# Reordering the steps of the delta-rule inverses and of attention among the matrix products of a two-layer hybrid mixer

## The chip, the cores and the metric

The kernel runs on one core of one Trainium2 chip. The metric is device time in microseconds (us) for one execution of the whole program, which is two layers and the final norm. The kernel before takes 1586.25 us, the median of three runs (1586.24 to 1587.02).

The engines are named as in the profile: PE multiplies matrices, PEld loads its weights, DVE is the vector engine, ACT the scalar engine, POOL the general one, SP issues DMAs. Each engine works through its own list of instructions in the order in which the built program holds them, and waits on semaphores for the others.

## The reference, cut to what matters

Two layers of a backbone over 256 latent tokens and 256 context tokens of width 1024. Each layer projects the normalised tokens once into column groups that feed three mixers: a Fourier branch, a bidirectional gated delta rule, and differential attention. The mixers are projected, merged by gates, and followed by a squared-ReLU MLP. The change touches the order of the work of two mixers.

```python
# delta rule, per chunk of 64 tokens, head and direction
gcum = jnp.cumsum(g, axis=-1)
decay = jnp.exp(jnp.where(lower, gcum[..., :, None] - gcum[..., None, :], -jnp.inf))
lmat = jnp.where(strict, jnp.einsum('nbhid,nbhjd->nbhij', kb, kc) * decay, 0.0)
tmat = lax.linalg.triangular_solve(eye + lmat, eye, left_side=True, lower=True, unit_diagonal=True)
u = tmat @ (vc * bc)
w = tmat @ (kb * jnp.exp(gcum)[..., None])
qk = jnp.einsum('nbhid,nbhjd->nbhij', qc, kc) * decay
def step(s, xs):
    v_new = u_i - w_i @ s
    out = qd_i @ s + qk_i @ v_new
    s = s * jnp.exp(gl_i)[..., None, None] + jnp.einsum('bhcd,bhce->bhde', ke_i, v_new)
# differential attention
s = jnp.einsum('bqhmd,bkhmd->bhmqk', q, k) * (DA_QK_DIM ** -0.5)
p = jax.nn.softmax(s, axis=-1)
a = p[:, :, 0] - lam * p[:, :, 1]
o = jnp.einsum('bhqk,bkhe->bqhe', a, v)
```

## The kernel before

**Dense products.** Nearly all of PE's time goes to weight products in float32 that are split into a high and a low half (`whi`, `wlo`, cast by ACT at L254 and subtracted by DVE at L255; the tokens are `hh`, `hl`), three products for each tile (`mm3`). They need no result of the chains below, and so can stand between the steps of a chain while ACT and DVE prepare the next step.

**Weave and chains.** `Weave` counts the time of these products as they are emitted (`weave.time`, columns divided by 2400 a microsecond, four passes for float32) and remembers, for each, its place in the scheduler's priorities. A chain of dependent small steps is emitted later inside `weave.chain()`: `at(t)` gives all that follows the priority of the product that stood at product time `t`. A step at `t0 + lat` thus goes `lat` microseconds of products behind the step at `t0`, and past the last product it simply follows. The scheduler then settles each engine's order, by these priorities and by what is ready in its own model.

**The delta-rule chain.** Four heads are taken as two pairs, in two layers: four chains, `dn_chain`, each with a step distance `lat` from `LAT` (1.2 and 1.0 us in layer 0, 0.6 and 0.6 in layer 1). A chain calls `prepare` twice, for two of its four chunk steps each, and then `step` four times. `prepare` has three parts. `products` multiplies k by k and k by q and copies the result to `gq` (DVE L663, ACT L666). Then, for each of its two steps `i`, come the decay: eight ACTIVATEs write the log rows `rh` and `rl` (L713, one buffer each), five products turn them into differences in a bank `pd` (`negr`, `rh`, `rl`), ACT takes the exponential `dec` (L721), DVE makes `C32` with four instructions (L723), ACT casts it to `C16` (L725, both are shown as `C` in the trace), POOL adds the identity, and DVE multiplies `dec` by `gq`. Last, at `2 * lat`, seven levels of a recursive inverse: the products of `C16` with `Tm`, DVE's mask `X` (L745), the products of `X` with `Um`, DVE's sum into `Tm` (L754), a transposition on PE and ACT's copy `Um` (L758); after the levels `T32`, `E16` and `U32` refine the result (L763 to L776). `step` forms `R`, multiplies it by `U32`, and makes `vs`, `vn`, the output and the new `state`.

**Attention.** `attention` handles a head in three groups of queries (two in layer 1). For each it places the scores (`km`, `q`), `CORE[0]` = 2.4 us later four transposes of `pe` and ACT's copy `aT` (L1045), `CORE[1]` = 0.8 us later the products of `aT` with the values `vt` and ACT's copy `od` (L1051), and after `CORE[2]` = 0.6 us the next group; at the end the norm of `od` (DVE L1061), its transposes and `yh`, `yl`.

**Beside them** in layer 0, pair 0 and in layer 1, pair 0 the Fourier branch `fnet` runs: its result banks are split into `u` (ACT and DVE L275, L276) and multiplied with the cosine table `ct`.

Of the kernel before, what the change touches and what calls it, by code (L numbers as in the profile page):

```python
# [11 lines left out]
F32 = mybir.dt.float32  # L12
F32R = mybir.dt.float32r
F16 = mybir.dt.float16
I32 = mybir.dt.int32
AF = mybir.ActivationFunctionType
# [18 lines left out]
LAT = ((1.2, 1.0), (0.6, 0.6))  # L35
POST = (5.0, 4.0)
GATE = (1.0, 9.0)
CORE = (2.4, 0.8, 0.6, 5.0)
NRM = (1.4, 3.0)

EARLY = 3
# [140 lines left out]
def body(tc, A, dbg=None):  # L182
    nc = tc.nc
    weave = Weave(tc)
    V, S, G, PE = nc.vector, nc.scalar, nc.gpsimd, weave
# [177 lines left out]
    tri = [kc[:, K_TRI + d * P:K_TRI + (d + 1) * P] for d in range(2)]  # L363
# [102 lines left out]
    def mixer(l, last, front):  # L466
# [11 lines left out]
        gates = {}  # L478
# [170 lines left out]
        def dn_chain(p, q2, k2, ktm, vtm, since, lat):  # L649
# [4 lines left out]
            def products(t):  # L654
                ps = dbank()
                withq = t < 2 or not last
                for h in range(2):
                    kt_ = k2[:, h, t * P:(t + 1) * P]
                    PE.matmul(ps[:, h * P:(h + 1) * P], kt_, kt_, start=True, stop=True)
                    if withq:  # L660
                        PE.matmul(ps[:, (2 + h) * P:(3 + h) * P], kt_, q2[:, h, t * P:(t + 1) * P], start=True, stop=True)
                o = dp.tile([P, 4, P], F32, tag="gq", name="gq", bufs=2)
                V.tensor_tensor(out=o[:, 0:2], in0=ps[:, 0:256].rearrange("p (a b) -> p a b", b=P),  # L663
                                in1=kc[:, K_NOT:K_NOT + P].unsqueeze(1).broadcast_to([P, 2, P]), op=ALU.mult)
                if withq:
                    S.copy(o[:, 2:4], ps[:, 256:512].rearrange("p (a b) -> p a b", b=P))  # L666
                return o

            def quad(nm, dt=F32, bufs=1, w=P):
                return dp.tile([P, 4, w], dt, tag=nm, name=nm, bufs=bufs)  # L670
# [17 lines left out]
            units = [(d, h) for d in range(2) for h in range(2)]  # L688

            def prepare(steps, t0):  # L690

                def at_(t):
                    nonlocal t0
                    t0 += t
                    at(t0)

                def part(t, i):

                    return t.rearrange("p (d s h) b -> p d s h b", d=2, s=2)[:, :, i]

                want = FWD[steps[0]] < 2 or not last
                at_(0)
                gq = {t: products(t) for t in sorted(FWD[s] for s in steps)}
                at_(lat)
                C32, C16 = (dp.tile([P, 8, P], t_, tag=nm, name=nm) for t_, nm in ((F32, "C32"), (F16, "C16")))
                decs = []
                for i, s in enumerate(steps):
                    tiles = (FWD[s], BWD[s])
                    rh, rl = quad("rh", F32R), quad("rl", F32R)
                    for u, (d, h) in enumerate(units):  # L710
                        for r_, g_ in ((rh, gates["ghi"].bitcast(F32)), (rl, gates["glo"])):
                            g_ = g_[:, d, s, 2 * p + h:2 * p + h + 1]
                            S.activation(r_[:, u], tri[d], AF.Copy, scale=g_)  # L713
                    pD = dbank()
                    PE.matmul(pD.rearrange("p (d h b) -> p d h b", d=2, b=P), idr, negr.unsqueeze(2).broadcast_to([P, 2, 2, P]), start=True, stop=False)
                    for d in range(2):
                        for j, r_ in enumerate((rh, rl)):
                            PE.matmul(pD[:, d * 256:(d + 1) * 256], strir[:, d], flat(r_)[:, d * 256:(d + 1) * 256],
                                      start=False, stop=d == 1 and j == 1)
                    dec = quad("dec", F32, 3)  # L720
                    S.activation(flat(dec), pD, AF.Exp)  # L721
                    for u, (d, h) in enumerate(units):
                        V.scalar_tensor_tensor(out=C32[:, 4 * d + 2 * i + h], in0=gq[tiles[d]][:, h],  # L723
                                               scalar=beta[:, d, s, 2 * p + h:2 * p + h + 1], in1=dec[:, u], op0=ALU.mult, op1=ALU.mult)
                    S.copy(part(C16, i), part(C32, i))  # L725
                    G.tensor_tensor(out=part(C32, i), in0=part(C32, i),
                                    in1=ident.unsqueeze(1).unsqueeze(1).broadcast_to([P, 2, 2, P]), op=ALU.add)
                    if want:
                        for d in range(2):
                            V.tensor_tensor(out=dec[:, 2 * d:2 * d + 2], in0=dec[:, 2 * d:2 * d + 2], in1=gq[tiles[d]][:, 2:4], op=ALU.mult)  # L730
                    decs.append(dec)


                at_(2 * lat)
                Tm, Um = (dp.tile([P, 8, P], F16, tag=nm, name=nm) for nm in ("Tm", "Um"))
                G.tensor_copy(Tm, id8)
                G.tensor_copy(Um, id8)
                for lv_ in range(NLVL):
                    w_ = 1 << lv_
                    tc_, uc_ = every_second(Tm, w_, 0), every_second(Um, w_, 1)  # L740
                    pX = dbank()
                    for u in range(8):
                        PE.matmul(pX[:, u * 64:(u + 1) * 64], C16[:, u], every_second(Tm, w_, u // 4, u), start=True, stop=True)
                    X = dp.tile([P, 8, 64], F16, tag="X", name="X")
                    V.tensor_tensor(out=X.rearrange("p (d h) b -> p d h b", d=2), in0=pX.rearrange("p (d h b) -> p d h b", d=2, b=64),  # L745
                                    in1=lvl[:, lv_].unsqueeze(2).broadcast_to([P, 2, 4, 64]), op=ALU.mult)
                    new = flat(X)
                    at_(lat)
                    if lv_:
                        new = dbank()  # L750
                        for u in range(8):
                            PE.matmul(new[:, u * 64:(u + 1) * 64], Um[:, u], X[:, u], start=True, stop=True)
                        at_(lat)
                    V.tensor_tensor(out=tc_, in0=new.rearrange("p (d b c) -> p d b c", d=2, c=w_), in1=tc_, op=ALU.add)  # L754
                    pU = dbank()
                    for u in range(8):
                        PE.matmul(pU[:, u * 64:(u + 1) * 64], Tm[:, u], every_second(id16, w_, 1 - u // 4, 0), start=True, stop=True)
                    S.copy(uc_, pU.rearrange("p (d b c) -> p d b c", d=2, c=w_))  # L758
                index = [[4 * d + 2 * i + h for d, h in units] for i in range(2)]
                pRs, U32s = [], []  # L760
                for i in range(2):
                    T32 = quad("T32", F32)
                    S.copy(T32.rearrange("p (d h) b -> p d h b", d=2), part(Tm, i))  # L763
                    pR = dbank()
                    for u, v in enumerate(index[i]):
                        PE.matmul(pR[:, u * P:(u + 1) * P], C32[:, v], T32[:, u], start=True, stop=True)
                    pRs.append(pR)
                for i in range(2):
                    at_(lat)
                    E16 = quad("E16", F16)  # L770
                    V.tensor_tensor(out=E16, in0=ident.unsqueeze(1).broadcast_to([P, 4, P]), in1=b4(pRs[i]), op=ALU.subtract)
                    pR = dbank()
                    for u, v in enumerate(index[i]):
                        PE.matmul(pR[:, u * P:(u + 1) * P], E16[:, u], Um[:, v], start=True, stop=True)
                    U32 = quad("U32", F32, 3)
                    V.tensor_tensor(out=U32.rearrange("p (d h) b -> p d h b", d=2), in0=pR.rearrange("p (d h b) -> p d h b", d=2, b=P),  # L776
                                    in1=part(Um, i), op=ALU.add)
                    U32s.append(U32)
                at_(lat)
                return t0, [(U32s[i], decs[i], want) for i in range(2)]  # L780
# [222 lines left out]
        def attention(h, qk, ap_, gain, cos, sin):  # L1003

            q, km, t0 = qk
            vt = vals[h]
            t0 = max(t0 + CORE[3], core_end[0])
            weaving = weave.chain()
# [4 lines left out]
            for ts in ((0,), (1,), (2, 3))[:2 if last else 3]:  # L1013
# [22 lines left out]
                for i in range(ng):  # L1036
                    sl = slice(i * wt, (i + 1) * wt)
                    V.scalar_tensor_tensor(out=pe[:, 0, sl], in0=pe[:, 1, sl], scalar=z[:, i:i + 1], in1=pe[:, 0, sl], op0=ALU.mult, op1=ALU.add)
                t0 += CORE[0]
                at(t0)  # L1040
# [61 lines left out]
        at_ = attention_pool()  # L1102
# [410 lines left out]
```

## Time and profile before

| what | value |
|---|---|
| median of the three runs | 1586.25 us |
| the profiled execution | 1584.71 us, of which its span is 1582.6 us |
| PE busy | 1517.0 us, 96% of the span |
| PEld, DVE, ACT, POOL busy | 82%, 74%, 46%, 9% |
| granted TensorE clock, mean | 0.99 of full speed |

The profiled execution lies 1.54 us below the median. PE is busy in nearly every slice of the span, but the ends of matmuls are modelled, so that short waits can hide in its busy time; what PE waited for is read from the list of waits and, place by place, from the timeline, where the bracket behind an instruction gives the idle time before it and what ended it. The chains lie in four stretches of the span: about 125 to 230 us and 300 to 432 us in layer 0 (pair 0, pair 1), 1040 to 1176 us and 1176 to 1330 us in layer 1.

### The profile page before, as it was taken

The page shows a single profiled execution, that of the slowest core. Times are in us where ns is not written, and L with a number is a line of the kernel's source. Part 1 is how long each engine was busy: PE and PEld are TensorE (multiplying, and loading weights), DVE is VectorE, ACT ScalarE, POOL GpSimd, SP SyncE. Part 2 cuts the span into 40 slices and gives each one's busy share as a digit, 9 for nine tenths or more (in the row PEclk, how much of TensorE's full clock was granted, in tenths as well). Part 3 has the DMA queues.
Part 4 walks back from the last instruction along what each step waited for, and adds up shares of the span by engine and source line. Part 5 has one row for each costly group of instructions (what it writes and reads, how often), then busy time and mean ns, then how long its engine had stood idle before and what let it go on. Part 6 is the DMA issues. An engine that isn't in the chain of part 4 may idle for free. (4 is left out here: it accounts for less than half of the span.)

```text
span 1582.6 us, 26109 instructions
## 1 busy us (share of the span) xinstructions
PE 1517.0 (96%) x10114; PEld 1305.2 (82%) x10114; DVE 1166.3 (74%) x2246; ACT 735.4 (46%) x1527; POOL 145.0 (9%) x173
## 2 busy tenths in 40 slices
PE   5899999999999999999999998899999999999997
PEld 2588888777888878888888888888988899999997
DVE  8787774768789797867676755776777886877765
ACT  3475533676532233423223233575457644555543
POOL 3400100011000012000000004001111100100001
PEclk9999999999999999999999999899999999999998
DMA  7532124211257573566566542141332135655662
GB/s 237 192 97 67 35 75 124 82 48 35 80 187 226 189 237 109 164 193 195 181 196 186 186 148 86 56 150 48 111 103 68 42 106 186 188 175 184 190 185 93
DMA packets 64461, 215.31 MB, mean 136 GB/s; under 512 B 7281, under 2 KB 12305, under 8 KB 64081
## 3 DMA queue, kind: packets, MB, share of 16 engines
q1 hardware_dynamic: 58178, 201.96, 40.7%
q10 hardware_dynamic: 5184, 7.21, 1.4%
q0 software_dynamic: 976, 4.48, 1.0%
q8 instruction: 79, 1.29, 0.4%
q14 instruction: 44, 0.36, 0.1%
HBM read 209.42 MB, written 4.20 MB: 135 GB/s over the span
## 5 line engine op out<-in xcount | busy, mean ns | idle before, releaser
L254 ACT CAST whi<-raw 128x1024 fp32r<-128x1024 f32 x277 | 290.5, 1050 | 220.6 <-PE pg L158 98.5
L255 DVE TENSOR_TENSOR wlo<-raw,whi 128x1024 fp32r<-128x1024 f32 x269 | 329.7, 1226 | 80.1 <-ACT whi L254 71.3
L158 PE MATMUL pg<-hh,whi 128*128 128x512 f32 (+1 forms) x856 | 304.0, 355 | 0.2
L158 PE MATMUL pg<-hh,wlo 128*128 128x512 f32 (+1 forms) x856 | 302.9, 354 | 0.5 <-DVE wlo L255 0.5
L158 PE MATMUL pg<-hl,whi 128*128 128x512 f32 (+1 forms) x856 | 303.1, 354 | 0.0
L336 DVE CUSTOM_DVE_ANT_0 junk<-raw,cb 128x1024 f16<-128x1024 f32 x128 | 157.0, 1227 | 57.8 <-DMA raw<-in_wt 56.3
L158 PEld LDWEIGHTS pg<-hh,whi 128*128 128x128 f32 x856 | 162.7, 190 | 20.6 <-issue 0.8
L158 PEld LDWEIGHTS pg<-hl,whi 128*128 128x128 f32 x856 | 162.8, 190 | 19.5 <-issue 0.8
L158 PEld LDWEIGHTS pg<-hh,wlo 128*128 128x128 f32 x856 | 162.7, 190 | 19.1 <-DVE wlo L255 0.7
L158 PE MATMUL pg<-a,whi 128*128 128x256 f32 (+1 forms) x448 | 107.5, 324 | 0.1
L435 POOL TENSOR_TENSOR acc<-acc,sq 128x256 f32<-128x256 f32 x36 | 38.1, 1067 | 661.7 <-ACT sq L433 661.7
L632 DVE SCALAR_TENSOR_TENSOR cy<-cu,conv,cy 128x512 f32<-128x512 f32 (+1 forms) x96 | 69.3, 723 | 30.3 <-ACT cy L630 29.0
L158 PEld LDWEIGHTS pg<-a,whi 128*128 128x128 f32 x448 | 75.8, 188 | 7.7 <-DVE a L276 0.8
L158 PE MATMUL pg<-a,wlo 128*128 128x256 f32 (+1 forms) x224 | 72.1, 322 | 0.0
L878 ACT ACTIVATE gt<-pg 128x256 f32<-128x256 f32 (+1 forms) x43 | 21.0, 488 | 102.6 <-PE pg L158 99.3
L158 PE MATMUL pd<-a,whi 128*128 128x512 f32 (+1 forms) x224 | 56.7, 334 | 0.1
L158 PE MATMUL pa<-hh,whi 128*128 128x512 f32 (+1 forms) x152 | 54.5, 358 | 1.0 <-ACT cy L630 0.9
L158 PE MATMUL pa<-hh,wlo 128*128 128x512 f32 (+1 forms) x152 | 54.0, 355 | 0.0
L158 PE MATMUL pa<-hl,whi 128*128 128x512 f32 (+1 forms) x152 | 53.6, 353 | 0.0
L1235 DVE TENSOR_TENSOR mr<-mr 128x512 f32<-128x512 f32 (+1 forms) x64 | 35.4, 555 | 23.6 <-ACT mr L1234 23.6
L158 PE MATMUL pg<-whi,hh 128*128 128x256 f32 (+1 forms) x160 | 50.9, 318 | 0.7 <-DVE q L996 0.5
L158 PE MATMUL pg<-wlo,hh 128*128 128x256 f32 (+1 forms) x160 | 50.1, 314 | 0.0
(444 smaller groups left out, 3611.4 us busy)
## 6 DMA issues: line engine op xcount, KB each, us to landing
raw<-in_wck SPq DMA_DIRECT2D x280, 512.0 KB, 3.6
raw<-in_wt SPq DMA_DIRECT2D x80, 512.0 KB, 3.6
wv<-in_wt SPq DMA_DIRECT2D x10, 512.0 KB, 4.1
wn<-in_wn SPq DMA_DIRECT2D x16, 192.0 KB, 3.7
x<-in_xin SPq DMA_DIRECT2D x4, 512.0 KB, 8.2
spill<-gt ACTq DMA_DIRECT2D x8, 256.0 KB, 3.9
cb<-crow POOLq DMA_DIRECT2D x2, 1024.0 KB, 7.0
merged<-spill ACTq DMA_DIRECT2D x8, 256.0 KB, 4.6
```

What stands on the lines that cost most here:

```text
L158: ins = self.pe.matmul(out, a, b, start=start, stop=stop)
L254: S.copy(hi, r)
L255: eng.tensor_tensor(out=lo, in0=r, in1=hi.bitcast(F32), op=ALU.subtract)
L336: V.tensor_tensor_reduce(out=junk, in0=r, in1=self.cb[:, v], scale=0.5, scalar=0.0, op0=ALU.mult, op1=ALU.add, accum_out=ada[l][:, n, v:v ...
L435: G.tensor_tensor(out=self.acc[s], in0=self.acc[s], in1=q, op=ALU.add)
L632: V.scalar_tensor_tensor(out=y3, in0=u[:, 0:ns, j:j + L], scalar=conv[:, f, j:j + 1], in1=y3, op0=ALU.mult, op1=ALU.add)
L878: S.activation(th, ps[:, :n], AF.Tanh, scale=0.5)
L1235: V.tensor_tensor(out=t, in0=t, in1=t, op=ALU.mult)
```

## The change

`CORE[1]`, the distance from attention's transposes to its value products, goes from 0.8 to 1.4. In `prepare` the eight ACTIVATEs of the log rows become a function `logs(s)`. Those of the first step are now emitted first, at the start of the preparation; the k and q products follow at `2 * lat`, the decay of both steps at `3 * lat` (the second step's log rows inside its loop, as before), and the levels at `6 * lat`, where they stood at `3 * lat`. No instruction is added or taken away; only the order changes, and the positions of the chains' steps between the products: all that follows a preparation is `3 * lat` later by the count, and each group of queries in attention takes 0.6 us more of product time, so that a head's third group starts 1.2 us later by the count.

```diff
--- before.py
+++ after.py
@@ -35,7 +35,7 @@
 LAT = ((1.2, 1.0), (0.6, 0.6))
 POST = (5.0, 4.0)
 GATE = (1.0, 9.0)
-CORE = (2.4, 0.8, 0.6, 5.0)
+CORE = (2.4, 1.4, 0.6, 5.0)
 NRM = (1.4, 3.0)
 
 EARLY = 3
@@ -699,18 +699,24 @@
                     return t.rearrange("p (d s h) b -> p d s h b", d=2, s=2)[:, :, i]
 
                 want = FWD[steps[0]] < 2 or not last
+                def logs(s):
+
+                    rh, rl = quad("rh", F32R), quad("rl", F32R)
+                    for u, (d, h) in enumerate(units):
+                        for r_, g_ in ((rh, gates["ghi"].bitcast(F32)), (rl, gates["glo"])):
+                            S.activation(r_[:, u], tri[d], AF.Copy, scale=g_[:, d, s, 2 * p + h:2 * p + h + 1])
+                    return rh, rl
+
                 at_(0)
+                ahead = logs(steps[0])
+                at_(2 * lat)
                 gq = {t: products(t) for t in sorted(FWD[s] for s in steps)}
                 at_(lat)
                 C32, C16 = (dp.tile([P, 8, P], t_, tag=nm, name=nm) for t_, nm in ((F32, "C32"), (F16, "C16")))
                 decs = []
                 for i, s in enumerate(steps):
                     tiles = (FWD[s], BWD[s])
-                    rh, rl = quad("rh", F32R), quad("rl", F32R)
-                    for u, (d, h) in enumerate(units):
-                        for r_, g_ in ((rh, gates["ghi"].bitcast(F32)), (rl, gates["glo"])):
-                            g_ = g_[:, d, s, 2 * p + h:2 * p + h + 1]
-                            S.activation(r_[:, u], tri[d], AF.Copy, scale=g_)
+                    rh, rl = logs(s) if i else ahead
                     pD = dbank()
                     PE.matmul(pD.rearrange("p (d h b) -> p d h b", d=2, b=P), idr, negr.unsqueeze(2).broadcast_to([P, 2, 2, P]), start=True, stop=False)
                     for d in range(2):
@@ -731,7 +737,7 @@
                     decs.append(dec)
 
 
-                at_(2 * lat)
+                at_(3 * lat)
                 Tm, Um = (dp.tile([P, 8, P], F16, tag=nm, name=nm) for nm in ("Tm", "Um"))
                 G.tensor_copy(Tm, id8)
                 G.tensor_copy(Um, id8)
```

Behind the changed lines the line numbers of the new kernel are larger by 6 (X is L751, Tm L760). In the lists of instructions below, `x4` is a repetition and a number behind a name a buffer; `LDWEIGHTS` of the small 16-bit products stand apart.

PE in layer 0, pair 0, where the first level of the inverse (`Tm,C`) meets the Fourier branch (`ct,u`; `u_1176` is the high half of u, `u_1177` the low one, `pa<-whi` are dense products). Before:

```order
L158 MATMUL pd<-Tm,C_1956 128x64
L158 MATMUL pa<-whi,hh 128x512
L158 MATMUL pa<-whi,hl 128x512
L158 MATMUL pa<-wlo,hh 128x512
L158 MATMUL pa<-whi,hh 128x512
L158 MATMUL pa<-whi,hl 128x512
L158 MATMUL pa<-wlo,hh 128x512
L158 MATMUL pg<-ct_1040,u_1176 128x256
L158 MATMUL pg<-ct_1040,u_1177 128x256
L158 MATMUL pg<-ct_1041,u_1176 128x256
L158 MATMUL pg<-ct_1040,u_1176 128x256
```

After:

```order
L158 LDWEIGHTS C_1966
L158 MATMUL pd<-Tm,C_1966 128x64
L158 MATMUL pg<-ct_1040,u_1176 128x256
L158 MATMUL pg<-ct_1040,u_1177 128x256
L158 MATMUL pg<-ct_1041,u_1176 128x256
L158 MATMUL pg<-ct_1040,u_1176 128x256
L158 MATMUL pg<-ct_1040,u_1177 128x256
L158 MATMUL pg<-ct_1041,u_1176 128x256
L158 MATMUL pg<-ct_1040,u_1176 128x256 x2
L158 MATMUL pg<-ct_1040,u_1177 128x256
L158 LDWEIGHTS Tm
```

The six dense products that stood between the level's products and the Fourier products are gone from there: they now stand ahead of the level.

DVE at the same place (`u` is the split of one token tile, `X` and `Tm` belong to the level). Before:

```order
L745 TENSOR_TENSOR X<-pd,lvl 128x512
L276 TENSOR_TENSOR u_1177<-pg,u_1176 128x512
L754 TENSOR_TENSOR Tm<-X,Tm 128x2x256
L276 TENSOR_TENSOR u_1177<-pg,u_1176 128x512
L276 TENSOR_TENSOR u_1177<-pa,u_1176 128x512
```

After:

```order
L276 TENSOR_TENSOR u_1177<-pg,u_1176 128x512
L751 TENSOR_TENSOR X<-pd,lvl 128x512
L276 TENSOR_TENSOR u_1177<-pg,u_1176 128x512
L760 TENSOR_TENSOR Tm<-X,Tm 128x2x256
L276 TENSOR_TENSOR u_1177<-pa,u_1176 128x512 x2
```

`X` now stands between the first two splits, where it stood ahead of both.

PE in layer 1, pair 0, the second step's log rows in the first preparation (`strir` is the triangle they are multiplied with). Before:

```order
L158 MATMUL pd<-rl,strir 128x256
L158 MATMUL pd<-rh,strir 128x256
L158 MATMUL pd<-rl,strir 128x256
L158 MATMUL pd<-negr,idr 128x512
L158 MATMUL pg<-ct_9792,u_9878 128x256
L158 MATMUL pd<-rh,strir 128x256
L158 MATMUL pg<-ct_9792,u_9879 128x256
```

After, the products of `rh` and `rl` that belong to the second `negr`, 22 rows behind it:

```order
L158 MATMUL pg<-ct_9792,u_9879 128x256
L158 MATMUL pg<-ct_9793,u_9878 128x256
L158 MATMUL pa<-z_9897,cc_9798 128x260
L158 MATMUL pd<-rh,strir 128x256
L158 MATMUL pa<-z_9897,cc_9799 128x260
L158 MATMUL pd<-rl,strir 128x256
L158 LDWEIGHTS C_10557
L158 MATMUL pd<-Tm,C_10557 128x64
```

The second `rh` product followed its `negr` by one Fourier product; now twenty of them and one of the next kind (`z,cc`) stand between.

PE in layer 1, pair 0, a product of `X` behind the level's product. Before, in the second preparation:

```order
L158 LDWEIGHTS C_10857
L158 MATMUL pd<-Tm,C_10857 128x64
L158 LDWEIGHTS C_10857
L158 MATMUL pd<-Tm,C_10857 128x64
L158 LDWEIGHTS Um
L158 MATMUL pd<-X,Um 128x64
L158 LDWEIGHTS Um
L158 MATMUL pd<-X,Um 128x64
```

After, in the first preparation (the place of before has dense products between the two again):

```order
L158 LDWEIGHTS C_10557
L158 MATMUL pd<-Tm,C_10557 128x64
L158 LDWEIGHTS C_10557
L158 MATMUL pd<-Tm,C_10557 128x64
L158 LDWEIGHTS Um
L158 MATMUL pd<-X,Um 128x64
L158 LDWEIGHTS Um
L158 MATMUL pd<-X,Um 128x64
```

The two kinds of product stand next to each other at one place of this chain before, and at another one now.

## Rows read from the trace of the kernel before

**Rows 1.** Waits of PE, whole span: in total (us), times, longest (us).

```profile
PE pc L166 <- DVE cy L637: 5.8, 3, 3.6
...
PE pd L158 <- ACT C L725: 2.2, 3, 0.9
...
PE pa L158 <- ACT aT L1045: 1.6, 3, 0.7
PE pd L158 <- ACT Um L758: 1.6, 2, 0.9
...
PE pd L158 <- ACT rh L713: 1.1, 1, 1.1
...
PE pd L158 <- ACT gq L666: 0.8, 1, 0.8
```

**Rows 2.** Windows of the chains: us; busy PE, PEld, DVE, ACT, POOL; clock, DMA share, GB/s.

```profile
125.00:230.00 105.00, 103.70 (x915) 88.38 (x914) 74.88 (x160) 59.05 (x141) 11.71 (x10) 1.00 0.18 54
300.00:432.00 132.00, 128.62 (x1039) 104.95 (x1038) 98.04 (x227) 79.67 (x209) 12.68 (x15) 1.00 0.18 57
1040.00:1176.00 136.00, 130.84 (x1129) 116.29 (x1128) 100.22 (x216) 76.52 (x177) 21.26 (x23) 0.99 0.32 98
1176.00:1330.00 154.00, 147.88 (x1311) 131.24 (x1309) 122.03 (x277) 91.34 (x213) 13.22 (x14) 1.00 0.30 92
```

**Rows 3.** Timeline of PE, layer 1, pair 0: start, us, [idle before <-releaser].

```profile
1060.98 0.39 PE L158 MATMUL pd<-rh,strir 128*128 128x256 f32 x1 [1.07 <-ACT rh L713]
```

**Rows 4.** Timeline of PE, layer 0, pair 1: later products of the first level.

```profile
326.60 0.35 PE L158 MATMUL pd<-Tm,C 128*128 128x64 f16 x6 [0.91 <-ACT C L725]
```

**Rows 5.** Timeline of PE, layer 0, pair 1: the scores of the second preparation.

```profile
362.78 0.50 PE L158 MATMUL pd<-negr,idr 128*128 128x512 f32 x1 [0.77 <-ACT gq L666]
```

**Rows 6.** Timeline of PE, layer 1, pair 0: a product of X.

```profile
1113.68 0.41 PE L158 MATMUL pd<-X,Um 128*128 128x64 f16 x8 [0.89 <-ACT Um L758]
```

**Rows 7.** Timeline of PE, layer 0, pair 0: first level beside the Fourier branch.

```profile
140.92 0.35 PE L158 MATMUL pd<-Tm,C 128*128 128x64 f16 x6
...
141.64 0.39 PE L158 MATMUL pa<-wlo,hh 128*128 128x512 f32 x1
141.88 0.40 PE L158 MATMUL pa<-whi,hh 128*128 128x512 f32 x1
```

**Rows 8.** Timeline of DVE at the same place.

```profile
141.31 0.69 DVE L745 TENSOR_TENSOR X<-pd,lvl 128x512 f16<-128x512 f32 x1 [0.57 <-PE pd L158]
141.92 0.68 DVE L276 TENSOR_TENSOR u<-pg,u 128x512 fp32r<-128x512 f32 x1
```

**Rows 9.** Timeline of ACT, layer 1, pair 1: log rows of a second inverse.

```profile
1244.02 0.60 ACT L721 ACTIVATE dec<-pd 128x512 f32<-128x512 f32 x1
...
1246.56 0.39 ACT L713 ACTIVATE rl<-kc,glo 128x128 fp32r<-128x128 f32 x1
```

**Rows 10.** Timeline of DVE, layer 1, pair 1: X, then od of attention.

```profile
1267.73 0.68 DVE L745 TENSOR_TENSOR X<-pd,lvl 128x512 f16<-128x512 f32 x1
...
1268.91 0.43 DVE L1061 TENSOR_TENSOR od<-od,roy 128x256 f32<-128x256 f32 x1
```

**Rows 11.** Timeline of DVE, layer 1, pair 0: a step of the state.

```profile
1146.86 1.22 DVE L255 TENSOR_TENSOR wlo<-raw,whi 128x1024 fp32r<-128x1024 f32 x1
1147.99 0.68 DVE L818 TENSOR_TENSOR vn<-pc,beta 128x512 f32<-128x512 f32 x1
```

**Rows 12.** Timeline of ACT, layer 1, pair 1: a weight cast ahead of od.

```profile
1214.22 1.04 ACT L254 CAST whi<-raw 128x1024 fp32r<-128x1024 f32 x1
1215.15 0.27 ACT L1051 COPY od<-pa 128x128 f32<-128x128 f32 x1
```

**Rows 13.** Timeline of PE, layer 1: the longest wait of the chain stretches.

```profile
1167.79 0.89 PE L166 MATMUL pc<-kc,cy 128*128 128x128 f32 x4 [1.99 <-DVE cy L637]
```

**Rows 14.** Windows round that wait, columns as in Rows 2.

```profile
1165.00:1170.00 5.00, 3.01 (x17) 2.71 (x16) 3.51 (x5) 2.92 (x7) 0.16 (x3) 0.81 0.33 105
1170.00:1175.00 5.00, 5.00 (x28) 4.51 (x28) 3.38 (x9) 3.06 (x12) 0.00 (x0) 0.85 0.33 105
```

## The prediction

> **What bounds the kernel now.** I read the page's busy times first. PE is busy for 96% of the span, and no instruction is added or removed, so PE's own work stays as it is. What the change can move is the time that PE waits. Second I read the list of what PE waited for. Its long entries, as the 5.8 us for `cy`, belong to steps that the change does not touch; the reader is to see how little is left for the chains: `C` 2.2 us, `aT` 1.6, `Um` 1.6, `rh` 1.1, `gq` 0.8, together 7.3 us [rows 1]. Third, the four stretches in which the chains run, by windows: PE lacks 1.3, 3.4, 5.2 and 6.1 us of them, 16 us in all, at a clock of 0.99 to 1.00, while DVE is busy for 71 to 79% and ACT for 56 to 60% [rows 2]. So a change of order can win a handful of microseconds at most, less than 0.5% of the time. Last I read the timeline at each of these waits, and beside it the new order: how many products now stand between the product that starts a step's work on ACT or DVE and the product that needs its result. I call the time of these products the lead. A wait is the step's latency less its lead. A product of 512 columns starts 0.24 us behind the one before it [rows 7], one of 256 columns I take at half of that.
>
> **What the change takes away.** These are places where a wait is in the trace and the lead grows.
> - The second step's `rh` in layer 1, pair 0: PE stood for 1.07 us [rows 3]. One product lay between; now it is 21. The wait goes: -1.1.
> - The cast `C` in layer 0, pair 1: PE stood for 0.91 us [rows 4]. From the last product of the log rows to the six products that wait, the lead goes from 2.4 to 4.1 us. Of the other two waits for `C` one gains 0.1 us and one (0.8) keeps its lead: -1.0.
> - `gq` in layer 0, pair 1: the lead grows by 0.66 us, the wait is 0.77 [rows 5]: -0.7.
> - `Um` in layer 1, pair 0, where the products of `X` stand right behind those of the level: 0.89 us [rows 6], and over a microsecond of dense products now stands between: -0.9.
> - `aT`: the larger distance would clear all of its 1.6 us [rows 1] if the transposes stood where the count puts them. In the new order they mostly come later than that, because `pe` is not ready in the scheduler's model; the mean lead of `aT` goes from 0.98 to 1.10 us only, and of its waits two gain 0.3 and 0.2 us: -0.5.
>
> Together -4.2 us. With all of it gone that could go (`aT`, `gq` and the smaller waits for `C` in full) it would be about -5.5.
>
> **What it brings.** The trace of before has no wait at these places; I bound each from below by no wait at all (the engine may come to the step earlier than it did) and from above by the latency of the same step in the trace, with whatever stood ahead of it on its engine.
> - The Fourier branch in layer 0, pair 0. `X` now stands on DVE between the first two splits of `u`, and `X` waits for the level's products. Queued behind it are the second split, `Tm` and two more splits, and the products `ct,u` on PE wait for the second split. The level's six products start at 140.92 and `X` at 141.31 [rows 7, 8], 0.2 us behind their end; `X` holds DVE for 0.6 us until the next start, the split takes 0.68 [rows 8]: about 1.5 us in all. Four products of 256 columns stand between, 0.5 us. I take +1.0; from 0 to 2.3, if a `wlo` of 1.22 us [rows 11] gets in between.
> - The products of `X` in layer 1, pair 0 now stand right behind the level's products at another place: the same wait of 0.89 us as in [rows 6], about half of which I let fall together with a shorter wait for `q` that stands close behind it: +0.4, from 0 to 0.9.
> - The log rows of the second inverse in layer 1, pair 1. They have one buffer, so ACT writes them when the first step's products have read it: the exponential, then eight ACTIVATEs, from 1244.02 to the end of the last at 1246.95, 2.9 us [rows 9]. The lead falls from 3.0 to 2.0 us: +0.9, from 0 to 1.6.
> - The transposes of `od` in layer 1, pair 1. On DVE the norm of `od` stands behind an `X`; from the start of that `X` to the end of the norm it is 1.6 us [rows 10], and the lead behind the products which `X` waits for falls from 2.5 to 1.1: with what is between the products and `X`, +0.8, from 0 to 1.9.
> - A step of the state in layer 1, pair 0: `vn` starts behind a `wlo` of 1.22 us and ends 1.8 us behind the start of it [rows 11]. The leads of `vn` and of `vs` fall from 1.9 and 1.8 to 0.9 and 1.0: +1.0, from 0 to 1.5.
> - The scores `km,q` at two places stand 0.45 us behind the value products, where they stood 1.0 and 1.4 behind. They need the bank that the copy of `od` frees, and that copy is short (0.27) but stands behind a weight cast of 1.04 on ACT [rows 12]: +0.6, from 0 to 1.9.
> - The levels. `X` takes 0.68 us and some 0.2 of signalling, as in [rows 6, 8]. Of the 48 places where products wait for it the mean lead falls from 1.26 to 1.11 us; many in layer 1 now have 0.91, enough if DVE is free and 0.6 short if it has a split in hand. It is busy for three quarters of the time [rows 2], but a wait at one level gives the next its lead back. I take one place in six at 1.1 us in sum: +1.0, from 0 to 3.
> - `T32`, `E16` and the rest, each with a few tenths less: +0.5, from 0 to 1.5.
>
> Together +6.2, from about 0 to 14, the upper end if all came at once. The ACTIVATEs that move ahead, eight in each of eight preparations, cost nothing by themselves: ACT has 40% of these stretches free [rows 2]. That each chain ends later (by 3 `lat` for each preparation, 3.6 to 7.2 us) costs nothing either: by the count of products 80 us and more stand behind every chain's end. In layer 0 the last steps of three heads of attention pass the last product of the count and simply follow; I leave them at nothing, from 0 to the 0.5 us that I gave the rest above. Without the cover each step would cost its latency of 1 to 2 us. POOL's and SP's lists are hardly touched.
>
> **The sum.** -4.2 + 6.2 = +2.0 us, made against the profiled execution of 1584.71 us (span 1582.6 and 2.1 around it). That execution lies 1.54 us below the median, and I carry the difference over: 1586.25 + 2.0 = **1588.3 us**.
>
> **The rivals.**
> - *The new short leads are covered.* For it: the steps of the four chains stand at hundreds of places, the leads of before were short at many of them too, and only ten waits come of it [rows 1]. Against it: the steps stand in a fixed row on DVE, and `X` ahead of a split cannot be passed. Then only about 1 us of the 6.2 comes, and the time is 1586.25 - 4.2 + 1.0 = 1583.1, or 1582 with the larger gain.
> - *Slower: DVE's order at the short leads.* At the Fourier branch, the levels and the norm of `od`, a step that waits for PE stands ahead of one for which PE waits. Each such pair costs the full latency once the lead is under `X` plus one split, 1.3 us [rows 8]. If most of the upper ends come (+11 to +12 of 14) the time is 1586.25 - 4.2 + 11.5 = 1593.6. It decides from about +7.4, where the loss passes 0.2%. Against it: waits in a row share one another, and the 7.3 us of all chain waits in the trace [rows 1] would have to double.
> - *The clock.* Behind the longest wait of the chain stretches, 2.0 us for `cy` [rows 13], the granted clock was 0.81 and 0.85 in the two windows of 5 us that hold it and what follows [rows 14], that is down to 1.2 GHz for a part of them: 0.19 x 5 + 0.15 x 5 = 1.7 us of PE's work. Behind the waits of 0.8 to 1.1 us the clock stayed, as the stretches' 1.00 shows [rows 2]. If three of the new waits reach 2 us the price is 3 x 1.7 on top: 1588.3 + 5.1 = 1593.4. The Trainium skill, page "TensorE: Matmul & The Clock Gate", section "A second HAM failure mode: psum-queue depth-cycling", speaks against orders with many short pauses: PE micro-idles between groups of matmuls made the clock swing between its levels. By that rule the time would be on this rival's side; the trace agrees only for the pause of 2.0 us and not for the shorter ones.
> - *The distance does what it says.* If `aT` really gets 0.6 us more everywhere, all 1.6 us of its waits go and not 0.5: 1587.2, inside the forecast.
>
> **How the numbers follow.** The forecast, a trade with little left over, has 0.54, of which 0.38 within 0.2% (3.2 us, about what a measurement of this kernel can tell from no change), 0.14 slower and 0.02 faster. Covered leads have 0.25: 0.17 faster by more than that, 0.08 within. DVE's order has 0.16 and the clock 0.05, all of it slower. In sum 0.19 faster, 0.46 the same, 0.35 slower. The range runs from the covered case (1583) to the slower ones (1594); beyond it I leave two in ten.
>
> **What would show it.** In the list of PE's waits after the change `rh` should be gone, `C` down to about one wait of 0.8 us, `gq` near nothing, and `aT` still there with about 1 us. New entries should be `u` or `z` of the split at L276 (0.5 to 2 us), `X` (from nearly nothing to 1 us or more), `od` and `vn`. In the windows the stretch from 300 to 432 us should gain a microsecond or two and the last one, layer 1, pair 1, lose two to three. If the new entries are missing, the covered case holds; if `X`, `Tm` and `u` have 7 us or more, DVE's order decides; a clock under 0.98 in one of the four stretches would be the third. The prediction is wrong at its root if the waits for `rh`, `C` and `Um` are still there, since the new order then does not give the lead that I read from it.

## The result, and the profile after

The changed kernel takes 1597.8 us (median of five runs, 1594.8 to 1600.7), against 1585.2 for the kernel before in the same comparison: a ratio of 1.0082, with a 95% interval of 1.0068 to 1.0096. A sixth run took 3822.9 us, is marked as slow and is left out. The kernel is **slower by about 13 us**. The forecast was 1588.3, within a range up to 1594.0. The profiled execution of the changed kernel has a span of 1594.5 us, 11.9 more than before.

The loss is in the chains, and a part of it is not in waits. These are the four chain stretches by windows, once for each kernel; their borders are the same dense products in both, to half a microsecond (columns as in [rows 2]). Before:

```profile
95.00:265.00 170.00, 168.48 (x1230) 142.12 (x1229) 116.06 (x268) 90.20 (x223) 12.26 (x18) 1.00 0.25 79
265.00:500.00 235.00, 231.03 (x1511) 188.36 (x1510) 183.91 (x375) 124.03 (x306) 13.21 (x23) 1.00 0.32 103
1034.00:1160.00 126.00, 122.83 (x1110) 110.08 (x1109) 93.61 (x204) 71.95 (x164) 18.36 (x18) 1.00 0.35 106
1160.00:1330.00 170.00, 161.89 (x1377) 143.26 (x1375) 133.56 (x294) 100.16 (x237) 16.13 (x19) 0.99 0.29 91
```

After:

```profile
95.00:270.00 175.00, 172.54 (x1230) 142.81 (x1229) 116.01 (x269) 89.46 (x222) 11.60 (x18) 1.00 0.25 75
270.00:508.50 238.50, 231.66 (x1510) 188.35 (x1509) 182.23 (x372) 125.42 (x306) 14.01 (x23) 1.00 0.32 101
1042.50:1169.00 126.50, 122.31 (x1107) 109.53 (x1105) 95.63 (x204) 71.65 (x164) 15.89 (x18) 1.00 0.34 105
1169.00:1341.40 172.40, 163.81 (x1378) 144.93 (x1379) 133.48 (x294) 100.80 (x237) 15.12 (x19) 0.98 0.30 91
```

The stretches grew by 5.0, 3.5, 0.5 and 2.4 us, 11.4 of the 11.9. What PE lacks of them went from 1.5, 4.0, 3.2 and 8.1 to 2.5, 6.8, 4.2 and 8.6 us, so 5.3 us more waiting. The other 6 us stand in the busy column, and two stretches hold them. In layer 0, pair 0 the same 1230 matmuls took 168.5 us of busy time and now take 172.5, at a clock of 1.00 in both. In layer 1, pair 1 the busy time grew by 1.9 us while the granted clock fell from 0.99 to 0.98. There, behind two short waits, PE ran at the lower of its two levels (1.2 GHz) for a part of two windows:

```profile
1315.71 0.39 PE L158 MATMUL pg<-ydh,whi 128*128 128x256 f32 x1 [0.78 <-ACT ydh L275]
1316.97 0.58 PE L158 MATMUL pg<-hh,wlo 128*128 128x256 f32 x1 [0.76 <-DVE wlo L255]
```

```profile
1315.00:1320.00 5.00, 3.53 (x16) 3.33 (x17) 4.57 (x9) 0.96 (x3) 0.00 (x0) 0.63 0.38 105
1320.00:1325.00 5.00, 5.00 (x33) 5.00 (x33) 0.50 (x1) 1.72 (x3) 0.00 (x0) 0.68 0.33 105
```

That is 0.37 x 5 + 0.32 x 5 = 3.4 us of PE's work, where the same stretch lost 1.7 before [rows 14]. It belongs to this execution. Whether the change brings it is not shown: the mean clock was 0.987 to 0.991 in the five runs of the changed kernel and 0.986 to 0.995 in those of the kernel before.

What PE waited for after (total in us, times, longest), the lines that answer to [rows 1]:

```profile
...
PE pd L158 <- DVE Tm L760: 2.2, 4, 1.3
...
PE pa L166 <- DVE sso L872: 1.8, 1, 1.8
PE pg L158 <- ACT km L1004: 1.4, 2, 1.2
...
PE pd L158 <- DVE X L751: 1.3, 2, 0.8
...
PE pa L166 <- DVE pe L1044: 1.1, 3, 0.5
...
PE pc L158 <- DVE oD L834: 0.9, 1, 0.9
PE pc L158 <- DVE state L857: 0.9, 1, 0.9
...
PE pg L158 <- DVE u L276: 0.7, 2, 0.5
...
PE pa L158 <- ACT aT L1051: 0.7, 1, 0.7
...
PE pd L158 <- ACT gq L666: 0.4, 1, 0.4
PE pd L158 <- ACT rh L707: 0.4, 1, 0.4
...
PE pd L158 <- ACT Um L764: 0.2, 1, 0.2
...
PE pd L158 <- ACT C L731: 0.2, 1, 0.2
```

The waits that the change was expected to take went further than forecast in sum: `C` from 2.2 to 0.2, `Um` from 1.6 to 0.2, `aT` from 1.6 to 0.7, `rh` from 1.1 to 0.4, `gq` from 0.8 to 0.4, in all 5.4 us against 4.2. (`rh` and `gq` by themselves lost 0.4 and 0.3 us less than forecast. The `rh` wait of layer 1, pair 0 is gone, and the 0.4 is a new one in layer 0, pair 1.) But the list has filled with others, of which before had only `Tm` (0.5), `X` (0.4) and `km` (0.2).

Some of them are those that were forecast, on PE's timeline (start, busy us, idle before and what ended it): the Fourier branch behind the second split of `u`, the product of `X` behind its level, and the last `od` of layer 0.

```profile
143.09 0.74 PE L158 MATMUL pg<-ct,u 128*128 128x256 f32 x4 [0.27 <-DVE u L276]
144.28 0.86 PE L158 MATMUL pg<-ct,u 128*128 128x256 f32 x5 [0.46 <-DVE u L276]
...
1083.95 0.39 PE L158 MATMUL pd<-X,Um 128*128 128x64 f16 x8 [0.78 <-DVE X L751]
...
457.97 0.63 PE L166 MATMUL pa<-kc,od 128*128 128x128 f32 x4 [1.85 <-DVE sso L872]
```

The list of waits puts the last one down to `sso`, a small step of the norm; the product reads `od`, which DVE finished just ahead of `sso`. On DVE `od` stood behind modulation products (L336), one of which had itself waited for a DMA:

```profile
454.69 1.23 DVE L336 CUSTOM_DVE_ANT_0 junk<-raw,cb 128x1024 f16<-128x1024 f32 x1 [1.93 <-DMA raw<-in_wt]
...
457.14 0.69 DVE L1067 TENSOR_TENSOR od<-od,roy 128x512 f32<-128x512 f32 x1
```

### The profile page after: what moved, and what is told of

The parts are those of the page before. It is cut to its first block, busy times and chain, and to the rows that moved or that the text cites. A ratio compares the mean times of both kernels' runs of the same rounds, so it can differ in the third digit from the quotient of the medians.

```text
span 1594.5 us, 26119 instructions
## 1 busy us (share of the span) xinstructions
PE 1524.1 (96%) x10114; PEld 1308.5 (82%) x10114; DVE 1167.4 (73%) x2246; ACT 736.3 (46%) x1527; POOL 141.3 (9%) x173
## 5 line engine op out<-in xcount | busy, mean ns | idle before, releaser
L336 DVE CUSTOM_DVE_ANT_0 junk<-raw,cb 128x1024 f16<-128x1024 f32 x128 | 157.1, 1227 | 58.2 <-DMA raw<-in_wt 56.7
L751 DVE TENSOR_TENSOR X<-pd,lvl 128x512 f16<-128x512 f32 x56 | 38.4, 686 | 21.7 <-PE pd L158 21.0
```

The lines of the kernel that those rows point to most:

```text
L336: V.tensor_tensor_reduce(out=junk, in0=r, in1=self.cb[:, v], scale=0.5, scalar=0.0, op0=ALU.mult, op1=ALU.add, accum_out=ada[l][:, n, v:v ...
```

## The experiments

Each is timed against the kernel before on the same chip, and the ratio of the two is given with its 95% interval; microseconds are that ratio times the kernel before. The comparisons ran on several chips, so two experiments are compared by their ratios. A **cut** below is a place in PE's order where a group of the small 16-bit level products begins or begins again behind a dense or Fourier product: 92 in the kernel before, 132 in the changed one.

### One part of the change at a time

CORE alone:

```diff
-CORE = (2.4, 0.8, 0.6, 5.0)
+CORE = (2.4, 1.4, 0.6, 5.0)
```

> The kernel before with CORE[1] = 1.4 alone. Three theories. Leads: the loss of the change (+13 us in the median) sits in the delta-rule preparations, so this alone moves little, -0.5 for aT and +1 to +2 for the last od of layer 0 (whose wait grew from 0.4 to 2.0 us): +0 to +2, 1585 to 1587. Breaks: the groups of small 16-bit level products are cut apart by dense products 92 times in the order of before and 92 times here, against 132 in the changed kernel, so +0. Draw (any new order loses what was tuned): attention's steps all move, so it costs as much as half of the change, +4 to +7.

Measured: 1.0017 (1.0005 to 1.0030), +2.7 us; in its profile the stretch of layer 0, pair 1 is 2.9 us longer and the others are not. The preparations' part alone (the change with CORE back at 0.8):

> The changed kernel with CORE[1] back at 0.8, so the preparations' part alone. Leads: most of the loss, +9 to +12 us, 1594 to 1597, without the 2.0 us wait for od in layer 0. Breaks: 126 cuts in its order against 92, at 0.07 us each +2.4 us from that cause, visible as more PE busy time with the same number of instructions in layer 0, pair 0 (window 95 to 265 us). Draw: +6 to +9, about the same as the other halves.

Measured: 1.0067 (1.0048 to 1.0086), +10.6 us. The log rows ahead, with the distances of before (the edit against the changed kernel, its changed lines):

```diff
-CORE = (2.4, 1.4, 0.6, 5.0)
+CORE = (2.4, 0.8, 0.6, 5.0)
...
 at_(0)
 ahead = logs(steps[0])
-at_(2 * lat)
 gq = {t: products(t) for t in sorted(FWD[s] for s in steps)}
...
-at_(3 * lat)
+at_(2 * lat)
 Tm, Um = (dp.tile([P, 8, P], F16, tag=nm, name=nm) for nm in ("Tm", "Um"))
```

> The log rows ahead at the start of a preparation, all distances and CORE as before. Leads: the two ends of the decay step come earlier on ACT and nothing else moves, so within 2 us of before, 1584 to 1588. Breaks: 102 cuts, +0.7 us. Draw: a smaller move than the others, +1 to +5.

Measured: 0.9995 (0.9986 to 1.0005), **nothing**. The distances alone, log rows in the loop:

> The longer distances alone (k and q products at 2 lat, levels 3 lat behind the decay), log rows in the loop as before, CORE as before. Leads and breaks both put the loss here: +8 to +11 us, of which 125 cuts make +2.3. If the log rows ahead are what hurts, this stays within 3 us of before.

Measured: 1.0099 (1.0082 to 1.0117), +15.7 us, more than the whole change. So the distances carry the loss. With the log rows ahead as well, which is the preparations' part above, it is 5 us less. But the two intervals overlap, and the four runs with the distances alone had the lower mean clock (0.988 against 0.9905), so this gain is not shown. The two halves of the distances, in the kernel before:

```diff
-at_(2 * lat)
+at_(3 * lat)
 Tm, Um = (dp.tile([P, 8, P], F16, tag=nm, name=nm) for nm in ("Tm", "Um"))
```

> One half of the distances: only the levels go from 2 lat to 3 lat behind the decay, all else as before. If the larger distance inside a preparation is what hurts (the steps' ACT and DVE work meets other work, and the groups are cut apart: 100 cuts in its order against 92), +5 to +8 us. If the start of the preparation is what hurts, this moves the levels and all steps behind them by one lat only and stays within 3 us of before.

Measured: 1.0008 (0.9998 to 1.0018), nothing that can be told apart.

```diff
-at_(0)
+at_(2 * lat)
 gq = {t: products(t) for t in sorted(FWD[s] for s in steps)}
```

> The other half: the whole preparation begins 2 lat later, with every distance inside it as before. No step gets more or less lead by the count; only the place among the dense products is another. If distances are what hurts, within 3 us of before. If the place is what hurts (what the steps meet there; 115 cuts against 92, +1.6 us by itself), +6 to +10 us, most of it in layer 0.

Measured: 1.0027 (1.0017 to 1.0037), +4.3 us. The halves together should give 5 to 6 by their sum, and gave 15.7: **the parts don't add up**. A loss by step and by distance, as the prediction summed it, would. Nor do the cuts make up the difference: there are 125 of them with both halves, 100 and 115 with one. Last, the whole change in layer 1 alone (layer 0 with `0.8`, `at_(0)`, `at_(2 * lat)` and no rows ahead):

> The change (logs ahead, distances, CORE) in layer 1 alone, layer 0 as before. From the stretches of the changed kernel (+1.0 in pair 0, +2.0 in pair 1) it should cost +3, 1587 to 1589, and its order has 93 cuts against 92. If it costs nothing, all of the loss sits in layer 0, by the cuts and the late end; if it costs +6 or more, the stretches of one profile are no measure of the parts.

Measured: 1.0017 (1.0007 to 1.0027), +2.7 us. Most of the loss is layer 0's, as the windows say.

### The cut groups

In the changed kernel, layer 0, pair 0, PE's timeline shows how the products of one level stand among dense ones of the branch projection (`yh`, `yl`):

```profile
205.29 0.35 PE L158 MATMUL pd<-id,Tm 128*128 128x64 f16 x6
205.48 0.48 PE L158 MATMUL pg<-yl,whi 128*128 128x512 f32 x1
205.80 0.20 PE L158 MATMUL pd<-id,Tm 128*128 128x64 f16 x1
205.84 0.48 PE L158 MATMUL pg<-yh,whi 128*128 128x512 f32 x1
206.16 0.20 PE L158 MATMUL pd<-id,Tm 128*128 128x64 f16 x1
206.20 0.47 PE L158 MATMUL pg<-yh,wlo 128*128 128x512 f32 x1
206.52 0.20 PE L158 MATMUL pd<-Tm,C 128*128 128x64 f16 x1
```

The eight products of a group (29 ns apart when they stand together) come in pieces of 6, 1 and 1. From 205.84 to 206.20 one dense product and one small one take 0.36 us, where a dense product alone takes 0.24 [rows 7] and a small one 0.03: some 0.09 us more for each piece. My reading is that the way in which the places are given does it: each instruction of a group gets a priority one above the one before it, so a group that is ready at its place is dealt out among dense products with the same priorities, while a group that is late goes out in one piece. More distance would make more groups ready in the scheduler's model. The next experiment gives all products of a group the priority of the first (its edit in part):

```diff
+with weave.whole():
     for u in range(8):
...
+def whole(self):
+    first, inner = self.tc.cur_priority, self.matmul
+    def matmul(*args, **kw):
+        self.tc.cur_priority = first
+        return inner(*args, **kw)
```

> The changed kernel with each group of eight 16-bit level products held together (all of a group get the place of its first): 98 cuts instead of 132. Breaks: the 4 us more of PE busy time in layer 0, pair 0 go, and the time falls from 1598.8 to about 1595. Leads alone: the order of waits is nearly the same, so no change beyond 1.5 us.

Measured: 1.0044 (1.0029 to 1.0059), 6 us less than the changed kernel. The same place on PE, and the same stretch (171.4 us, where the changed kernel has 175.0):

```profile
205.31 0.39 PE L158 MATMUL pg<-yl,whi 128*128 128x512 f32 x1
205.55 0.41 PE L158 MATMUL pd<-id,Tm 128*128 128x64 f16 x8
205.79 0.47 PE L158 MATMUL pg<-yh,whi 128*128 128x512 f32 x1
206.11 0.41 PE L158 MATMUL pd<-Tm,C 128*128 128x64 f16 x8
```

```profile
95.00:266.40 171.40, 169.52 (x1231) 141.91 (x1229) 116.25 (x267) 89.12 (x221) 11.28 (x18) 1.00 0.24 78
```

PE's busy time there is 169.5 us and not 172.5, and 98 of the 132 cuts are left. In the kernel before the same edit has nothing to mend:

> The kernel before with the same holding together: 94 cuts against 92, so by the breaks no change, within 1.5 us of before. A move of more than 3 us either way would say that the order's draw, and not the cuts, is what such an edit changes.

Measured: 1.0002 (0.9993 to 1.0011). A second pair of kernels came from the redraw of the changed kernel that is told of below (146 cuts, 1.0063), with the groups held together:

> The changed kernel redrawn by 0.3 us earlier, now with the level groups held together: 108 cuts against 146, on which 1593.5 us were measured (ratio 1.0063). Cuts at about 0.1 us each: -4 us, ratio 1.003 to 1.005, the loss of a neutral redraw. If cuts are not what costs, the ratio stays at 1.006.

Measured: 1.0036 (1.0022 to 1.0049), 4 us less, though the two intervals overlap. The stretch of layer 0, pair 0, cut and whole:

```profile
95.00:271.20 176.20, 174.85 (x1231) 143.51 (x1230) 117.56 (x267) 89.75 (x223) 11.31 (x18) 1.00 0.24 76
```

```profile
95.00:268.00 173.00, 170.50 (x1230) 142.89 (x1229) 118.88 (x267) 88.94 (x223) 11.30 (x18) 1.00 0.24 77
```

174.9 us of busy time for 1231 matmuls became 170.5 for 1230, with the waits slightly up (1.4 to 2.5 us lacking). The price of one holds all over the trace of before: behind a level product the next start after a 512-column product comes 0.31 us later and not 0.23 (median of 40 places without a wait), after a 256-column one 0.20 and not 0.11 (65 places), and the first small product of a piece takes 0.01 more. In this stretch PE goes from a level product to a dense or Fourier one 26 times before and 62 times after, 32 times with the groups held together; in the redraw 81 and 37 times. At 0.1 us each that makes +3.6, -3.0 and -4.4 us, and the busy column moved by +4.1, -3.0 and -4.4. So **the cuts are a cause by themselves**: about 4 us of the 13, 40 more of them at 0.1 us. The timed gains of 6 and 4 us agree with this, but by their intervals they could be 3 to 9 and 0 to 8.

### Is it the late end?

In the changed kernel the chain of layer 0, pair 1 ends 14 us later, and its norm and the last `od` meet the next layer's modulation products on DVE. I put this pair's preparations back and kept the rest (groups held together).

> The changed kernel with its level groups held together, and with the preparations of layer 0, pair 1 alone put back to the order of before. Late end: this pair's chain ended 14 us later (its first sum of squares at 445.5 us against 431.0), so that its norm and the last od meet the next layer's modulation products on DVE (L336, 1.22 us each, which also wait for DMAs). Put back, the 3.5 us that this stretch lost go, and the time falls from 1592.8 to about 1589.5. Draw, or attention's share (the run with CORE alone lost 2.9 us in the same stretch): 1591 to 1593, the loss there stays.

Measured: 1.0064 (1.0048 to 1.0080), no gain; its profile still loses 3.7 us in that stretch, but at other waits (`Tm` 1.7, the products of `pe` 1.8 in two waits, `C` 0.9, and only 0.6 for the last `od`). **The late end as the cause falls**: with it gone the same time is lost elsewhere.

### A draw of the order

That left the question whether any move of the steps loses. Four kernels differ from the one before in one number that lengthens or shortens no step: every preparation begins 0.3 us of products later, 0.3 earlier, 0.6 later, or each head of attention begins 0.3 earlier. The diff shows the first edit and, apart from it, the last; the other two have -0.3 and 0.6 in the place of 0.3.

```diff
-at_(0)
+at_(0.3)
...
-CORE = (2.4, 0.8, 0.6, 5.0)
+CORE = (2.4, 0.8, 0.6, 4.7)
```

> The kernel before with every preparation begun 0.3 us of products later, and nothing else: a neutral redraw of the order (89 cuts against 92, the chains end 0.6 us later by the count). Draw: +3 us or more, as any new order loses what was tuned. Distance from the end and cuts: nothing, within 2 us of before.

> The kernel before with every preparation begun 0.3 us of products earlier. Draw (the order of before was found to be good, and any redraw loses): +2 to +6 us, as the shift of 0.3 us later did with +5. Later is worse: an earlier start gains or does nothing, -2 to +1. Cuts: 100 against 92, +0.6.

> The same with 0.6 us later. Draw: +2 to +6, no more than 0.3 us later gave. Later is worse: more than the +5.2 of 0.3 us, up to +8. Cuts: 96 against 92, +0.3.

> The kernel before with each head of attention begun 0.3 us of products earlier, the inverses untouched. Draw: +1 to +5. If what loses is the inverses' place alone: within 1.5 us of before.

Measured: 1.0033 (1.0021 to 1.0045), 1.0038 (1.0026 to 1.0049), 1.0032 (1.0019 to 1.0046) and 1.0024 (1.0010 to 1.0038): **each is slower by 4 to 6 us**, earlier as well as later, 0.6 no more than 0.3. Their profiles show it as waiting: PE's busy time is 1516.7 to 1518.3 us in the four (1517.0 before), and what PE lacks of the span is 67.3 to 70.8 us (65.6 before). The edits that cost nothing (log rows ahead, levels later, groups held together in the kernel before, and the last run below) lack 63.5 to 65.6. The waits of two of the four are listed here. With 0.3 later:

```profile
...
PE pg L158 <- ACT km L998: 2.4, 3, 1.3
...
PE pd L158 <- ACT C L725: 1.2, 2, 1.0
...
PE pg L158 <- DVE u L276: 1.2, 2, 0.8
...
PE pd L158 <- DVE X L745: 1.2, 3, 0.6
PE pa L166 <- DVE pe L1038: 1.0, 2, 0.8
```

With 0.3 earlier:

```profile
...
PE pd L158 <- ACT C L725: 3.0, 5, 0.9
PE pa L166 <- DVE od L1061: 2.9, 2, 2.7
...
PE pd L158 <- DVE Tm L754: 2.4, 4, 1.2
...
PE pd L158 <- DVE X L745: 1.5, 3, 0.9
...
PE pd L158 <- ACT rh L713: 1.0, 1, 1.0
...
PE pd L158 <- ACT Um L758: 1.0, 1, 1.0
```

In the first `rh` and `gq` are gone and `km`, `u` and `pe` are there; in the second `C` has grown to five waits and one `od` waits for 2.7 us. The changed kernel, redrawn in the same way:

> The changed kernel with every preparation 0.3 us earlier, its own redraw: 146 cuts against 132. Draw: a kernel that was not picked by its time moves either way, 1590 to 1600; cuts alone: +1.0 on 1598.8, 1599 to 1601.

Measured: 1.0063 (1.0040 to 1.0085) with more cuts (146). That is 3 us less than the changed kernel, where 14 more cuts alone would add 1.4, but the intervals overlap, so a change of its waits is not shown. Last, the two edits that had cost nothing, together:

> The log rows ahead with the distances of before, and the level groups held together: 98 cuts (102 without the holding, 92 before). It joins the two edits that cost nothing alone. If both are neutral, within 2 us of before; if either hid a gain, 1580 to 1582.

Measured: 0.9998 (0.9988 to 1.0009). No version beat the kernel before.

## Why the prediction was wrong

- **"No instruction is added or removed, so PE's own work stays as it is."** This step failed first. PE's list has the same instructions, but 40 more pieces of small products among dense ones, and that costs about 4 us of which the list of waits shows nothing. The sum had no term for it. It stood in the order of the changed kernel before any run: dense and level products in turn, one by one.
- **What it takes away, -4.2.** Right in kind, and too small: the five entries lost 5.4 us, also because `C` and `Um` lost waits in layer 1, pair 1 whose lead I had counted as unchanged. `aT` lost 0.9, between my 0.5 and the 1.6 of the rival that it would get its distance: both waits of layer 0, pair 1 went, and one of 0.7 stands in layer 1, pair 1, where it was 0.4.
- **What it brings, +6.2, from 0 to 14.** This step failed second, and by its size: inside its range, but 4 to 5 us above its value. PE lacks 5.3 us more in the stretches, so with 5.4 taken away some 10 to 11 us of new waits came. Of the places that I named, the split of `u` came nearly as priced (0.7 in the list, +1.0 forecast); `X` behind its level came at the upper bound (0.78 at 1083.95 for +0.4, with 0.9 as the bound), since the wait for `q` behind it, with which I let half of it fall, stayed at 0.5; and the last `od` of layer 0 came with 1.85, which I had left at "nothing to 0.5". The log rows of the second inverse in layer 1, pair 1, the `od` of that pair, `vn` and `km,q` brought no entry of their own size. In their place stand `Tm` (2.2, four times), `km` (1.4, dense products whose bank ACT's copy `km` frees), `pe` (1.1), `oD`, `state`. My reading of this: I listed the places where the lead fell below the latency *of the trace of before*, and that latency is itself a result of the order, of what stands ahead on DVE and ACT at that moment. It is seen at the last `od`, which stood behind a DMA's 1.93 us on DVE; for the other new waits it is not shown one by one.
- **The chains' later end "costs nothing".** The last `od` shows that it is not free, but putting the end back won nothing.
- **The rivals.** DVE's order, which I gave 0.16, was nearest in sign and size, but not by its mechanism: its sign was 7 us or more at `X`, `Tm` and `u`, and they have 4.2; the waits are of a dozen kinds. The covered case was wrong. The clock's rival priced single pauses of 2 us. In the profiled execution the clock fell behind waits of 0.78 and 0.76 us instead and cost 1.7 us more than before, a third of its 5.1; no stretch was under 0.98, the sign that I gave. The rule that many short pauses make it swing (the Trainium skill, "TensorE: Matmul & The Clock Gate", section "A second HAM failure mode: psum-queue depth-cycling") is borne out at this one place; in the other three stretches the clock stayed at 1.00 with waits up to 1.85 us. Nor does a wait settle it here. PE stood 1.30 us for `wlo` until 1307.1 us in the kernel before, and 1.30 us for the same `wlo` until 1305.2 in that kernel with its groups held together; behind it the clock stayed in the first and fell in the second:

```profile
1309.00:1314.00 5.00, 4.73 (x41) 4.73 (x42) 2.46 (x5) 1.76 (x3) 0.00 (x0) 1.00 0.84 258
```

```profile
1306.00:1311.00 5.00, 5.00 (x34) 5.00 (x33) 3.20 (x5) 0.76 (x1) 0.00 (x0) 0.70 0.82 225
```

- **The sum by terms.** The parts measured alone (-0.8, +1.3, +4.3, +2.7) come to 7.5 and the whole to 13. A forecast that adds place to place is open to an error of that size here.

What is shown: the cuts (two pairs of kernels, and the price of one in the trace), the neutral log rows, and that four of four small moves of the chains lose 0.24 to 0.38%. With the groups held together the changed kernel stands at 1.0044 and its redraw at 1.0036, near the level of these moves; with one pair put back it stood at 1.0064. So the likeliest reading is about 4 us for the cuts and the other 9 for an order that is not the one of before: 5.3 us of them are the longer waits of the profiled execution and 1.7 its clock, which other executions need not share. That the order of before is a good draw, with distances that suit it, is argued from these runs, not shown by itself; the log rows ahead and the levels one `lat` later also reorder PE's list and lost nothing, so not every move does.

## What to carry to other kernels

When a change only moves small steps between large ones, look at the new order for two things before counting leads: how often the engine in the middle switches between the kinds (each piece of a group that is dealt out costs about 0.1 us here), and whether a step's latency in the old trace would be the same at the new place. A kernel whose distances were chosen by timing may sit at a good draw of its order; so shift everything by a small neutral amount as well, and compare a change of the order with what that costs (here about 5 us, 0.3%). And look at the granted clock of a stretch before its busy time is put down to the order. Groups of small products should be held together by the planner, not by chance.

## What the runs showed of the hardware

A switch from the small 16-bit products to a dense one cost about 0.09 to 0.10 us beyond both products' own time, whole group or single product, 512 columns or 256: 205.79 to 206.11 in the kernel with whole groups is 0.32 us for one dense product, as behind the cut pieces. A weight load of a dense product takes 190 ns on PEld in the profile, far longer than a small product's 29 ns; that this is the reason was not tried. The profile books the loss as busy time of PE, not as a wait. It does the same with a lower clock: 0.63 and 0.68 of full speed in two windows of 5 us raised PE's busy time and not its waits. That fall came behind two waits of under 0.8 us, and a wait of 1.30 us was followed by a fall in one execution and by none in another.
